# Channel-major delta-rule keys scaled by a broadcast row of reciprocal norms, in place of transposed scaled tokens

## The chip, the cores and the metric

The kernel runs on one core of one Trainium2 chip. The metric is the device time of one execution in microseconds (us); the median of the runs shown is compared. The profile is of one execution of its own, with the span from the first to the last instruction.

## What is computed

One hybrid decoder layer over 512 tokens: a conditioned RMS norm, one wide input projection, a sliding-window attention branch, a gated delta-rule branch, a gated merge and an output projection. The change lies in the delta rule's keys. There are 16 key heads of 128 channels, shared by 32 value heads. Cut to what the keys need, in chunks of 64 tokens:

```python
d_qkv = causal_conv_silu(d_qkv, conv_w)
dq, dk, dv = jnp.split(d_qkv, [DN_KEY, 2 * DN_KEY], axis=-1)
dk = jnp.repeat(l2_norm(dk.reshape(B, T, DN_K_HEADS, DN_HEAD_K)), rep, axis=2)
...
def l2_norm(x):
    xf = x.astype(jnp.float32)
    return xf * lax.rsqrt(jnp.sum(xf * xf, axis=-1, keepdims=True) + EPS)
...
k_beta = k * beta[..., None]
L = jnp.where(strict, jnp.einsum('bhncd,bhnsd->bhncs', k_beta, k) * decay, 0.0)
t_inv = triangular_solve(eye + L, eye)
```

So each token's key is divided by its norm over the 128 channels, and the normed keys are multiplied with each other (K times K transposed), masked by a decay, and enter a triangular inverse.

## The kernel before, in words

Weights are streamed. Each projection tile (128 output channels by 512 tokens) takes 48 matmuls on TensorE: 16 slices of the input, each in three matmuls (L240 to L242) of weights and activations that are split into a high and a low part. A tile's weights come as one load of 1 MB into `raw` (two buffers, L200). ScalarE makes the high half `whi` (L52), VectorE the low half `wlo` (L53), in two halves per tile; three such halves are kept.

All else is written as Python generators that run beside the tiles. After every second slice, that is after six matmuls, `pump` advances the live generators by one count; `yield n` in a generator gives up n counts. This sets the order in which instructions are recorded. A list scheduler then places them on each engine's queue by its own estimate of readiness, so an instruction may stand somewhat earlier or later than recorded. Each engine runs its queue in order. All loads and stores are issued from one queue, SP's; a load or store whose semaphore isn't there yet holds up what stands behind it.

The change lies in `keys` (L651), one generator for each of the 16 key heads, numbered 0 to 15 here. Keys 0 to 3 come from tiles made during the start, 4 to 15 from their own projection tiles, with tiles of the merge gate between them from key 8 on. The steps of one key:

- the convolution with its activation gives `y`, 128 channels by 512 tokens, with channels in the partitions (L576 to L587);
- four transposes on TensorE bring the tokens into the partitions, `ptk` in PSUM (L274);
- ScalarE sums squares per token (L702), VectorE computes the reciprocal root `rky`, 128 tokens by 4 blocks, in ten small steps (L59 to L64);
- two rows `g_rows` are loaded, each broadcast to 128 partitions, as decay masks `E` (L707), which GpSimd completes with a sum and a selection (L714, L715);
- ScalarE scales the tokens to `k` (L668), which is stored to DRAM as `k_d` (L674);
- four more transposes bring `k` back to channels, `ptkT` in PSUM, and ScalarE copies it to `kT` (L676), which is stored as `kT_d` (L682);
- four matmuls of `kT` with itself give `pkk` (L681); VectorE multiplies it with the two masks (L687), and the results are stored as `lt_d` and `lab_d` (L694, L695).

When keys 0 to 7 are stored, their matrices are loaded as `A` and VectorE solves them, a long series of products and sums (L757, L764) that runs beside the later keys. After all keys the loop over heads reads `kT_d` and `k_d` back. In the rows of the profile "pkk x8" are one key's four matmuls, each of which the profile shows as two.

Of the kernel before, what the change touches and what calls it, by code (L numbers as in the profile page):

```python
# [7 lines left out]
F32 = mybir.dt.float32  # L8
# [3 lines left out]
ALU = mybir.AluOpType  # L12
# [4 lines left out]
P = 128  # L17
T = 512
# [4 lines left out]
KH = 16  # L23
# [13 lines left out]
class Layer:  # L37
# [552 lines left out]
    def deltanet(self):  # L590
        tc, nc, a = self.tc, self.nc, self.a
        dram = self.dram
        self.lt_d = dram.tile([2, 2, 16, 4, HD, HD], F32, name="lt_d")
        self.lab_d = dram.tile([VH, HD, 4, HD], F32, name="lab_d")
        self.ta_d = dram.tile([2, 16, 4, HD, HD], F32, name="ta_d")
        self.ts_d = dram.tile([2, 2, 16, 4, HD, HD], F32, name="ts_d")
        self.kT_d = dram.tile([KH, P, T], F32, name="kT_d")
        self.k_d = dram.tile([KH, P, T], F32, name="k_d")
        self.o_d = dram.tile([VH, P, T], F32, name="o_d")
        with ExitStack() as ps:  # L600
            self.pmm = ps.enter_context(tc.tile_pool(name="pmm", bufs=2, space=PSUM, reuse_waits="tile"))
            self.ptp = ps.enter_context(tc.tile_pool(name="ptp", bufs=2, space=PSUM, reuse_waits="tile"))
            self.gwk = ps.enter_context(tc.tile_pool(name="gwk", bufs=1, reuse_waits="tile"))
            sol1 = ps.enter_context(tc.tile_pool(name="sol1", bufs=1, side="right", reuse_waits="tile"))
            with ExitStack() as sa:
                wk = sa.enter_context(tc.tile_pool(name="dnA", bufs=2, reuse_waits="tile"))
                sol0 = sa.enter_context(tc.tile_pool(name="sol0", bufs=1, reuse_waits="tile"))
                gp = sa.enter_context(tc.tile_pool(name="gates", bufs=1, reuse_waits="tile"))
                self.go(self.gates(gp), 1)
                self.keys_done, self.solve_in = [], {}  # L610
                self.keep_order = True
                for g in range(NST):
                    self.go(self.keys(wk, g, self.acc_k[g]), 10 + 8 * g)
                for j in range(NFIRST):
                    self.merge_gate("mb", j, self.mb_d)
                self.go(self.solve_load(sol0, 0), 1)
                self.go(self.solve_load(sol1, 1), 1)
                s0 = self.paced(self.solve(sol0, 0, nc.vector), 0.82)
                s1 = self.paced(self.solve(sol1, 1, nc.vector), 0.0)
                for kind, j in self.mixed():  # L620
                    if kind == "k":
                        self.go(self.keys(wk, j, self.channel_tile(f"k{j}")), 0)
                    else:
                        self.merge_gate("mb", j, self.mb_d)
                        if j == KT - 3:
                            s0[1] = 1.2
                for j in range(3):
                    self.merge_gate("ma", j, self.ma_d)
                    if s0 not in self.slow:
                        s1[1] = 1.1  # L630
                self.drain_live()
                self.drain_slow(s0)
                self.keep_order = False
                s1[1] = 0.6
            with ExitStack() as sb:
                wk = sb.enter_context(tc.tile_pool(name="dnB", bufs=2, reuse_waits="tile"))
                self.tt = []
                for n in range(4):
                    t = wk.tile([P, NTB, P], F32, tag=f"tt{n}", name=f"tt{n}", bufs=1)
                    nc.gpsimd.memset(t[HD:P, :, 0:HD], 0.0)  # L640
                    self.tt.append(t)
                for g in range(KH):
                    if g == 8:
                        self.drain_slow(s1)
                    self.heads(wk, g)
                for j in range(3, 5):
                    self.merge_gate("ma", j, self.ma_d)
                self.drain_live()
        self.dump("o", self.o_d)

    def keys(self, wk, g, ps):  # L651

        nc = self.nc
        y = wk.tile([P, T], F32, tag="y", name="y", bufs=3)
        yield from self.conv(wk, ps, 16 + g, y)
        yield 2
        pt = self.ptp.tile([P, T], F32, tag="tp", name="ptk")
        self.transpose4(pt, lambda c: y[:, c * P : (c + 1) * P])
        ss = self.sumsq(wk, pt)
        yield 3  # L660
        self.hold = 2
        nc.vector.tensor_scalar(out=ss, in0=ss, scalar1=EPS, scalar2=None, op0=ALU.add)
        rk = self.rsqrt(wk, ss, NTB, "rk")
        E = [self.decay_load(wk, 2 * g + e) for e in range(2)]
        yield 2
        k = wk.tile([P, NTB, P], F32, tag="k", name="k")
        for c in range(NTB):
            nc.scalar.activation(k[:, c, :], pt[:, c * P : (c + 1) * P], AF.Copy, scale=rk[:, c : c + 1])  # L668
        for e in range(2):
            self.decay_mask(E[e], 2 * g + e)  # L670
        yield 3
        pt = self.ptp.tile([P, T], F32, tag="tp", name="ptkT")
        self.transpose4(pt, lambda c: k[:, c, :])
        nc.sync.dma_start(out=self.k_d[g], in_=k.rearrange("p c d -> p (c d)"))  # L674
        kT = wk.tile([P, T], F32, tag="kT", name="kT")
        nc.scalar.copy(out=kT, in_=pt)  # L676
        yield 2
        pk = self.ptp.tile([P, NTB, P], F32, tag="tp", name="pkk")
        for c in range(NTB):
            sl = slice(c * P, (c + 1) * P)  # L680
            nc.tensor.matmul(pk[:, c, :], lhsT=kT[:, sl], rhs=kT[:, sl], start=True, stop=True)  # L681
        nc.sync.dma_start(out=self.kT_d[g], in_=kT)  # L682
        for e in range(2):
            nc.scalar.activation(E[e], E[e], AF.Exp)
        yield 1
        for e in range(2):
            nc.vector.tensor_tensor(out=E[e], in0=pk, in1=E[e], op=ALU.mult)  # L687
        yield 2
        for e in range(2):
            h = 2 * g + e  # L690
            b, hl = h // 16, h % 16
            for k2 in range(2):
                s = slice(k2 * HD, (k2 + 1) * HD)
                nc.sync.dma_start(out=self.lt_d[b, k2, hl].rearrange("c j i -> j c i"), in_=E[e][s, :, s])  # L694
            nc.sync.dma_start(out=self.lab_d[h], in_=E[e][0:HD, :, HD:P])  # L695
        self.keys_done.append(g)
# [8 lines left out]
    def decay_load(self, wk, h):  # L705
        E = wk.tile([P, NTB, P], F32, tag="E", name="E", bufs=4)
        self.nc.sync.dma_start(out=E.rearrange("p c i -> p (c i)"), in_=self.g_rows[h].partition_broadcast(P))  # L707
        return E
# [859 lines left out]
```

## Time and profile before

| what | us |
|---|---|
| median of 3 runs | 2932.36 |
| lowest and highest run | 2931.61, 2937.2 |
| span of the profiled execution | 2929.7 |

The profile's page lists the busy time of the engines (PE is TensorE's matmuls, PEld its weight loads, DVE VectorE, ACT ScalarE, POOL GpSimd), then the chain of work that ended last. Rows of the timeline give the start in us, the duration in us, the engine, the line and operation, then output and inputs; brackets at the end give how long the engine had been idle and what released it. Matmuls overlap, so their durations add up to more than the time between their starts. Rows of groups give the busy time, the mean of one in ns, and the idle time before them with its releaser. SPq rows are the issue of a load or store on SP's queue.

The keys stand between about 160 and 500 us of the span.

### The profile page before, as it was taken

Reading aid. Unit: us, or ns where it says so; the run is one execution under the profiler, and the core shown is the slowest. Engines: PE = TensorE matmul, PEld = TensorE weight load, DVE = VectorE, ACT = ScalarE, POOL = GpSimd, SP = SyncE. Lnnn points to the kernel's source line nnn. Section 1 sums busy time; section 2 is a strip of 40 time slices with the busy share of each in tenths; the row PEclk is TensorE's granted clock in tenths of the full one; section 3 lists DMA queues with packets and bytes.
Section 4 is the critical chain, followed back from the end, with each engine's and each line's share of the span. In section 5 each row is a group of like instructions: output and inputs, shape, how many; then the busy total and the mean of one; then the engine's idle time right before and its main releaser. Section 6 shows DMA issues by size and latency. Waiting matters only on the chain.

```text
span 2929.7 us, 38073 instructions
## 1 busy us (share of the span) xinstructions
PE 2870.6 (98%) x14556; PEld 2351.2 (80%) x14556; DVE 1787.2 (61%) x2915; ACT 1085.1 (37%) x2113; POOL 243.0 (8%) x204
## 2 busy tenths in 40 slices
PE   8899999999999999999999999999999999999988
PEld 6677888888888888888888788888787877888867
DVE  6775998777776545544444553434655655553697
ACT  4355333333334333333333322212343443432343
POOL 0022211100000110000000000000100000000022
PEclk9999999999999999999999999999999999999999
DMA  9747555633334533333332675554322223375562
GB/s 387 281 147 219 163 169 159 203 109 111 125 113 134 160 116 124 115 122 109 123 109 100 235 263 182 186 172 141 105 89 94 85 89 103 119 262 172 173 194 97
DMA packets 175046, 451.11 MB, mean 154 GB/s; under 512 B 72433, under 2 KB 74993, under 8 KB 138897
## 3 DMA queue, kind: packets, MB, share of 16 engines
q1 hardware_dynamic: 174866, 448.70, 46.1%
q8 instruction: 114, 1.87, 0.3%
q14 instruction: 66, 0.54, 0.1%
HBM read 386.95 MB, written 59.45 MB: 152 GB/s over the span
## 4 chain that ended last, share of the span: by engine, by line
PE 84%; DVE 3%; DMA 2%; issue 1%; ACT 1%; POOL 1%; SPq 0%; POOLq 0%; DVEq 0%; ACTq 0%
PE mm L240 24%; PE mm L242 24%; PE mm L241 24%; DVE wlo L53 1%; PE S L1208 1%; PE pv L918 1%; PE po L937 1%; PE O L1259 1%; PE pP L274 1%; PE po L936 1%; PE pd L933 1%; PE pp L908 1%; PE m L241 1%; PE m L242 1%; PE m L240 1%
## 5 line engine op out<-in xcount | busy, mean ns | idle before, releaser
L240 PE MATMUL mm<-hh,whi 128*128 128x512 f32 x2784 | 1130.7, 406 | 2.3 <-ACT whi L52 1.6
L242 PE MATMUL mm<-hh,wlo 128*128 128x512 f32 x2784 | 1089.6, 391 | 1.3 <-DVE wlo L53 1.3
L241 PE MATMUL mm<-hl,whi 128*128 128x512 f32 x2784 | 1087.3, 391 | 0.0
L53 DVE TENSOR_TENSOR wlo<-raw,whi 128x1024 fp32r<-128x1024 f32 (+1 forms) x452 | 554.4, 1229 | 491.5 <-ACT whi L52 481.7
L52 ACT CAST whi<-raw 128x1024 fp32r<-128x1024 f32 (+1 forms) x452 | 470.7, 1044 | 972.9 <-PE mm L241 927.3
L242 PEld LDWEIGHTS mm<-hh,wlo 128*128 128x128 f32 x2784 | 522.6, 188 | 115.1 <-DVE wlo L53 2.2
L240 PEld LDWEIGHTS mm<-hh,whi 128*128 128x128 f32 x2784 | 523.7, 188 | 112.3 <-issue 8.4
L241 PEld LDWEIGHTS mm<-hl,whi 128*128 128x128 f32 x2784 | 524.2, 188 | 98.7 <-issue 0.4
L240 PE MATMUL mm<-oh,whi 128*128 128x512 f32 x512 | 200.6, 393 | 2.6 <-ACT oh L52 1.7
L242 PE MATMUL mm<-oh,wlo 128*128 128x512 f32 x512 | 199.4, 390 | 0.5 <-DVE wlo L53 0.5
L241 PE MATMUL mm<-ol,whi 128*128 128x512 f32 x512 | 199.5, 390 | 0.1
L865 POOL TENSOR_TENSOR qe<-qe,yq 128x512 f32<-128x512 f32 x32 | 51.4, 1624 | 902.7 <-DMA qe<-eg_rows 836.9
L714 POOL TENSOR_TENSOR E<-E,neg_g 128x512 f32<-128x512 f32 x64 | 78.4, 1224 | 476.2 <-DMA E<-g_rows 342.8
L240 PEld LDWEIGHTS mm<-oh,whi 128*128 128x128 f32 x512 | 96.0, 188 | 24.8 <-ACT oh L52 3.0
L241 PEld LDWEIGHTS mm<-ol,whi 128*128 128x128 f32 x512 | 96.1, 188 | 22.2 <-DVE ol L53 1.3
L764 DVE TENSOR_TENSOR A<-A,atmp 128x62 f32<-128x62 f32 (+30 forms) x124 | 112.9, 911 | 1.5
L242 PEld LDWEIGHTS mm<-oh,wlo 128*128 128x128 f32 x512 | 96.1, 188 | 20.9 <-DVE wlo L53 1.3
L757 DVE TENSOR_TENSOR atmp<-A 128x62 f32<-128x62 f32 (+30 forms) x124 | 109.3, 882 | 1.5
L911 DVE SCALAR_TENSOR_TENSOR r<-pp,neg_eg,vt 128x128 f32<-128x128 f32 x96 | 29.2, 346 | 78.8 <-PE pp L908 77.6
L1232 ACT ACTIVATE sm<-sm,mx,rs 128x256 f32<-128x256 f32 (+1 forms) x128 | 71.7, 561 | 3.3 <-DVE mx L1227 3.3
L580 DVE SCALAR_TENSOR_TENSOR yv<-mm,convh,yv 128x511 f32<-128x511 f32 (+2 forms) x96 | 71.5, 745 | 1.6
L241 PE MATMUL m<-wlo,hh 128*128 128x512 f32 x128 | 51.8, 404 | 10.1 <-DVE wlo L53 10.1
(331 smaller groups left out, 3145.6 us busy)
## 6 DMA issues: line engine op xcount, KB each, us to landing
raw<-in_w_ch SPq DMA_DIRECT2D x158, 1024.0 KB
wa<-in_w_ada_ss SPq DMA_DIRECT2D x32, 1024.0 KB
raw<-in_w_od SPq DMA_DIRECT2D x32, 1024.0 KB
E<-g_rows SPq DMA_DIRECT2D x64, 256.0 KB
gw<-in_w_ada_gate SPq DMA_DIRECT2D x16, 1024.0 KB
raw<-in_w_os SPq DMA_DIRECT2D x16, 1024.0 KB
qe<-eg_rows SPq DMA_DIRECT2D x32, 256.0 KB
o_d<-zh SPq DMA_DIRECT2D x32, 256.0 KB
```

What stands on the lines that cost most here:

```text
L52: self.nc.scalar.copy(out=hi, in_=src)
L53: self.nc.vector.tensor_tensor(out=lo, in0=src, in1=hi.bitcast(F32), op=ALU.subtract)
L240: nc.tensor.matmul(ps, lhsT=wh, rhs=xh, start=first, stop=False)
L241: nc.tensor.matmul(ps, lhsT=wh, rhs=xl, start=False, stop=False)
L242: self.last_mm = nc.tensor.matmul(ps, lhsT=wl, rhs=xh, start=False, stop=last).ins
L274: self.nc.tensor.transpose(dst[:, c * P : (c + 1) * P], src_cols(c), self.ident)
L580: nc.vector.scalar_tensor_tensor(out=y[:, s:], in0=ps[:, : T - s], scalar=w[:, j : j + 1], in1=y[:, s:], op0=ALU.mult, op1=ALU.add)
L714: nc.gpsimd.tensor_tensor(out=E, in0=E, in1=ng, op=ALU.add)
L757: eng.tensor_tensor(out=t, in0=A[:, m : m + 1, m + 1 :].to_broadcast([P, m, n]), in1=A[:, :m, m : m + 1].to_broadcast([P, m, n]), op=ALU.mult,
L764: eng.tensor_tensor(out=A[:, :m, m + 1 :], in0=A[:, :m, m + 1 :], in1=t, op=ALU.add)
L865: nc.gpsimd.tensor_tensor(out=qf, in0=qf, in1=q, op=ALU.mult)
L1232: nc.scalar.activation(t, t, AF.Exp, scale=r[:, h : h + 1], bias=mx[:, h : h + 1], accum_out=den[:, h : h + 1])
```

## The change

The channel-major key `kT` is no longer made by transposing the scaled tokens. `rk`, the reciprocal norms, is stored to a row of 512 numbers in DRAM, `r_d`, with tokens in order. That store has 512 pieces of one number each. The row is loaded back, broadcast to 128 partitions, into `kT`. GpSimd multiplies it in place with `y`, the unscaled channel-major key. The four transposes `ptkT`, their PSUM tile and ScalarE's copy are gone. The scaled tokens `k` are still made by ScalarE and stored. The store of `k` is recorded two counts after the scaling instead of three; the counts from the reciprocal root to `pkk` are seven, as before. The load of `kT` must wait for the store of `r_d`, which waits for the reciprocal root.

```diff
@@ deltanet
+        self.r_d = dram.tile([KH, T], F32, name="r_d")
@@ keys
         rk = self.rsqrt(wk, ss, NTB, "rk")
+        nc.sync.dma_start(out=self.r_d[g].rearrange("(c p) -> p c", p=P), in_=rk)
         E = [self.decay_load(wk, 2 * g + e) for e in range(2)]
+        kT = wk.tile([P, T], F32, tag="kT", name="kT")
+        nc.sync.dma_start(out=kT, in_=self.r_d[g].partition_broadcast(P))
         yield 2
         k = wk.tile([P, NTB, P], F32, tag="k", name="k")
         for c in range(NTB):
             nc.scalar.activation(k[:, c, :], pt[:, c * P : (c + 1) * P], AF.Copy, scale=rk[:, c : c + 1])
         for e in range(2):
             self.decay_mask(E[e], 2 * g + e)
+        yield 2
+        nc.gpsimd.tensor_tensor(out=kT, in0=kT, in1=y, op=ALU.mult)
+        nc.sync.dma_start(out=self.k_d[g], in_=k.rearrange("p c d -> p (c d)"))
         yield 3
-        pt = self.ptp.tile([P, T], F32, tag="tp", name="ptkT")
-        self.transpose4(pt, lambda c: k[:, c, :])
-        nc.sync.dma_start(out=self.k_d[g], in_=k.rearrange("p c d -> p (c d)"))
-        kT = wk.tile([P, T], F32, tag="kT", name="kT")
-        nc.scalar.copy(out=kT, in_=pt)
-        yield 2
         pk = self.ptp.tile([P, NTB, P], F32, tag="tp", name="pkk")
```

## The prediction

> **What bounds the kernel now.** I read the page first: busy time, then the chain of work that ended last. TensorE fills the span.
>
> ```profile
> span 2929.7 us, 38073 instructions
> PE 2870.6 (98%) x14556; PEld 2351.2 (80%) x14556; DVE 1787.2 (61%) x2915; ACT 1085.1 (37%) x2113; POOL 243.0 (8%) x204
> PE 84%; DVE 3%; DMA 2%; issue 1%; ACT 1%; POOL 1%; SPq 0%; POOLq 0%; DVEq 0%; ACTq 0%
> ```
>
> The reader is to see that work taken off TensorE's queue shortens the kernel one for one, and that any wait put into that queue lengthens it one for one. The edit lies between 160 and 500 us; in the built order of the changed kernel every engine's instructions from the query heads on stand as before. So only this stage counts. Its last stretch, from the table by stage (length in us, then PE, PEld, DVE, ACT and POOL busy):
>
> ```profile
> 450.00:500.00 50.00, 49.14 (x229) 40.37 (x228) 47.79 (x65) 18.86 (x36) 10.74 (x12) 1.00 0.55 165
> ```
>
> PE is nearly full, and so is DVE, which runs the triangular solve there and has 2 us in 50 left.
>
> **What is removed.** Sixteen keys lose four transposes each (ptkT) and a copy on ScalarE. The grouped rows of 160 to 500 us give ptkT's idle time, and POOL's price for the kind of product that is added:
>
> ```profile
> L274 PE MATMUL ptkT<-ident,k 128*128 128x128 f32 x64 | 12.1, 287 | 4.5 <-ACT k L668 4.3
> L714 POOL TENSOR_TENSOR E<-E,neg_g 128x512 f32<-128x512 f32 x32 | 43.7, 1365 | 403.9 <-DMA E<-g_rows 334.9 <-DVE rky L64 54.5 <-DMA k_d<-k 9.4
> ```
>
> Matmuls overlap, so the duration is not the price; the spacing is. Undisturbed matmuls start 0.227 us apart (three steps from 310.90 to 311.58); around four transposes it is 0.91 us from 300.87 to 301.78 for two steps.
>
> ```profile
> 300.87 0.40 PE L242 MATMUL mm<-hh,wlo 128*128 128x512 f32 x1
> 301.11 0.60 PE L274 MATMUL ptkT<-ident,k 128*128 128x128 f32 x4
> 301.46 0.48 PE L240 MATMUL mm<-hh,whi 128*128 128x512 f32 x1
> 301.78 0.40 PE L241 MATMUL mm<-hl,whi 128*128 128x512 f32 x1
> ...
> 310.90 0.39 PE L240 MATMUL mm<-hh,whi 128*128 128x512 f32 x1
> ...
> 311.58 0.39 PE L240 MATMUL mm<-hh,whi 128*128 128x512 f32 x1
> ```
>
> So four transposes cost 0.91 - 0.45 = 0.46 us, and sixteen keys 7.3 us. With them go the 4.5 us that PE stood idle before ptkT, waiting for ScalarE's scaled tokens. Together 11.8 us. The copy of kT on ScalarE (about 0.6 us each) saves nothing by itself: ScalarE is busy 37%. The freed PSUM buffer I count at nothing too, as no row shows a matmul waiting for it.
>
> **What is added, and where it waits.** Before, pkk needed rsqrt, scaling, transposes, copy. Now it needs rsqrt on DVE, a store of the row r_d, a load that waits on SP until the store has landed, and a product on POOL behind the two masks of the same key. PE is in order: if kT is late, pkk and all weight matmuls behind it stand. The prices, from the SP queue's rows, the chain and the timeline:
>
> ```profile
> 314.58 1.25 SPq L694 DMA_DIRECT2D lt_d<-E  x2
> 222.98 2.41 DMA lab_d<-E
> 2918.83 3.39 DMA x<-in_x
> 196.33 0.88 SPq L707 DMA_DIRECT2D E<-g_rows  x2
> 200.27 1.05 POOL L714 TENSOR_TENSOR E<-E,neg_g 128x512 f32<-128x512 f32 x1 [8.68 <-DMA E<-g_rows]
> 410.90 0.90 SPq L707 DMA_DIRECT2D E<-g_rows  x2
> 416.67 1.05 POOL L714 TENSOR_TENSOR E<-E,neg_g 128x512 f32<-128x512 f32 x1 [18.80 <-DMA E<-g_rows]
> ...
> 475.83 2.01 POOL L714 TENSOR_TENSOR E<-E,neg_g 128x512 f32<-128x512 f32 x1
> ```
>
> The store is of 512 single numbers. Two lt_d stores, 256 runs each, take 1.25 us to issue, a run being one contiguous piece; lab_d, 256 runs, lands 2.41 us after its issue began. With another 0.6 us of issue I take 3.05 us; below, 2.41 us; above, 4.2 us, about an E pair's landing. The load is the same shape as one of the E loads: the first of a pair is used 3.94 us after issue (196.33 to 200.27), 5.77 us when a weight load is ahead of it (410.90 to 416.67), and a plain load of that size took 3.39 us. I take 3.94, the same kind without company. The product: 1.37 us mean, 1.05 to 2.01 at the ends. With 0.15 us for the hand-overs, rsqrt's end to pkk needs 8.5 us; bounds 6.9 and 12.
>
> What is there for it? One undisturbed late key, with the last rsqrt step and pkk:
>
> ```profile
> 349.56 0.60 PE L274 MATMUL ptk<-ident,y 128*128 128x128 f32 x4
> 356.82 0.16 DVE L64 SCALAR_TENSOR_TENSOR rky<-rkt,rky 128x4 f32<-128x4 f32 x1
> 364.12 1.05 PE L681 MATMUL pkk<-kT 128*128 128x128 f32 x8
> ```
>
> 7.1 us, less 0.46 for the transposes that are gone: 6.7. Here the built order keeps pkk behind the same weight matmul as before. For others it moves pkk: counted in weight matmuls of 0.227 us, by +9, +8, -6, +6, +2, +8 for keys 0 to 5, by 39 to 52 for keys 6 to 8 and 36 for key 9, and by 0, 0, +7, 0, 0, +17 for keys 10 to 15. The rows of keys 0, 1, 2, 5, 14 and 15:
>
> ```profile
> 178.99 0.16 DVE L64 SCALAR_TENSOR_TENSOR rky<-rkt,rky 128x4 f32<-128x4 f32 x1
> 179.61 1.10 PE L274 MATMUL ptkT<-ident,k 128*128 128x128 f32 x4 [1.00 <-ACT k L668]
> 183.74 1.05 PE L681 MATMUL pkk<-kT 128*128 128x128 f32 x8
> 193.13 0.16 DVE L64 SCALAR_TENSOR_TENSOR rky<-rkt,rky 128x4 f32<-128x4 f32 x1
> 193.75 0.33 PE L274 MATMUL ptkT<-ident,k 128*128 128x128 f32 x1 [0.77 <-ACT k L668]
> 197.54 1.05 PE L681 MATMUL pkk<-kT 128*128 128x128 f32 x8
> 206.83 0.16 DVE L64 SCALAR_TENSOR_TENSOR rky<-rkt,rky 128x4 f32<-128x4 f32 x1
> 216.31 1.05 PE L681 MATMUL pkk<-kT 128*128 128x128 f32 x8
> 235.97 0.16 DVE L64 SCALAR_TENSOR_TENSOR rky<-rkt,rky 128x4 f32<-128x4 f32 x1
> 236.58 0.59 PE L274 MATMUL ptkT<-ident,k 128*128 128x128 f32 x2 [1.68 <-ACT k L668]
> 240.03 1.05 PE L681 MATMUL pkk<-kT 128*128 128x128 f32 x8
> 450.37 0.16 DVE L64 SCALAR_TENSOR_TENSOR rky<-rkt,rky 128x4 f32<-128x4 f32 x1
> 456.84 1.05 PE L681 MATMUL pkk<-kT 128*128 128x128 f32 x8
> 476.86 1.00 DVE L64 SCALAR_TENSOR_TENSOR rky<-rkt,rky 128x4 f32<-128x4 f32 x1
> 478.32 1.10 PE L274 MATMUL ptkT<-ident,k 128*128 128x128 f32 x4 [0.86 <-ACT k L668]
> 482.03 1.05 PE L681 MATMUL pkk<-kT 128*128 128x128 f32 x8
> ```
>
> Room is the gap from rsqrt's end to pkk, plus the move, less 0.46, less the idle in brackets (it goes, so PE is there sooner). Key 0: 4.59 + 2.04 - 0.46 - 1.00 = 5.2, so 3.3 us are missing. Key 1: 4.25 + 1.82 - 0.46 - 0.77 = 4.8; 3.7 missing. Key 2: 9.32 - 1.36 - 0.46 = 7.5; 1.0. Key 5: 3.90 + 1.82 - 0.46 - 1.68 = 3.6; 4.9. Key 14: 6.31 - 0.46 = 5.85; 2.65. Key 15: 4.17 + 3.86 - 0.46 - 0.86 = 6.7; 1.8. Keys 10 and 13 have key 11's distance and aren't moved: 1.8 each with it. For key 12 the move leaves 0.3, but its mask loads now stand behind the waiting store, and I take 1.5. Keys 3, 4 and 6 to 9 I put at nothing: 3 and 4 have key 2's distance and a move to the good, the others the longer one. Sum 12.9 for keys 0 to 5 and 11.4 for 10 to 15: 24 us of new standing on PE.
>
> The store waits on SP for rsqrt, the load for the store. Behind them stand kT_d, k_d, the next key's mask loads and weight loads. In the late part the weight loads wait anyway, for DVE to free a raw buffer:
>
> ```profile
> SPq L200 <- DVE wlo L53: 95.9, 15, 12.9
> ```
>
> (15 times between 150 and 540 us, up to 12.9 us). So I count nothing for SP; without that cover a weight load 3 to 4 us later per key would cost up to that. POOL's product may also hold DVE up: the last rsqrt step of key 15 took 1.00 us beside POOL work, 0.16 elsewhere, at most 16 x 0.85 = 13.6 us. PE's new waits give DVE that time back, so nothing.
>
> **The sum.** -11.8 + 24 = +12 us on the profiled 2929.7: a span of 2942. The median of the runs lies 2.7 us above that span, so about 2944 us. With the round trip at 6.9 us, each tight key stands 1.6 us less: about 9 us in all, net -3. At 12 us keys 2 to 4 join, about 60 us, net +48.
>
> **Rivals.**
> *The round trip hides* (faster). The order was built with a readiness for kT that put most pkk where they were; if that is right, nothing new stands, and -11.8 gives 2920.5 us. For it: keys 6 to 9 were moved far, so lateness was reckoned with. Against: keys 0, 1 and 5 have under 5.3 us, and the fastest two transfers seen already take 5.8 without the product.
> The Trainium skill ("DMA: Bandwidth & Descriptors", Anatomy of one DMA) gives a transfer about 2.0 us fixed plus its bytes at 436 GB/s; my estimate from it is 2.0 + 2.6 + 1.37 = 6.0 us, which leaves some 4 us of standing and about 2925 us. The same page (Specifications) says that pieces under 512 B cost a read-modify-write, which speaks for a slower store; no row here has a piece of 4 B.
>
> *SP becomes the bound in the middle* (slower). Keys 3 to 8 follow each other closely, and in the built order of that part the weight load stands right behind kT_d, which waits for POOL's product, and the mask loads that POOL needs first stand behind r_d, which waits for rsqrt. Decides if kT of keys 5 to 8 is more than about 5 us later than the order assumes; each weight tile late by 5 to 6 us, four tiles, adds 20 to 24 us: 2966 us. Against: the longer distance of pkk there moves with it.
>
> *Even* (no change that can be told). Store and load at their fast ends: -3, 2929 us.
>
> **How the numbers follow.** Forecast 0.55, hidden 0.13, SP 0.20, even 0.12. A change under about 0.2%, 6 us, can't be told from none. Faster: 0.14 (hidden, and a little of even). Same: 0.17 (the rest of even, the low edge of the forecast). Slower: 0.69. Predicted 2944. The range reaches down into even, 2925, and above over the SP case, 2970; the forecast's own is 2930 to 2962.
>
> **What would show it.** Right: PE's ptkT rows gone; idle before pkk, released by POOL's kT product, 15 to 30 us in about ten keys, largest at keys 0, 1, 5 and 14; r_d landing about 3 us after issue, the load about 4. Wrong in size: pkk idle under 8 us (hidden), or the store landing after 5 us or more. Wrong in kind: PE idle at the weight matmuls released by ScalarE's or DVE's split, which wait for raw loads (SP).

## The result and the profile after

| | kernel before | changed kernel |
|---|---|---|
| median of the runs, us | 2931.99 (4 runs, 2929.86 to 2937.2) | 3088.01 (4 runs, 3086.12 to 3090.3) |
| span of the profiled execution, us | 2929.7 | 3085.6 |

The changed kernel is slower: 1.0536 times the time of before, 95% interval 1.0521 to 1.0551. That is 156 us, where 12 were forecast.

The page of the changed kernel, first the busy time, then the granted clock in 40 slices (each digit is tenths of full speed), then the chain of work that ended last, by engine:

```profile
PE 2898.9 (94%) x14492; PEld 2373.6 (77%) x14492; DVE 1788.8 (58%) x2915; ACT 1078.3 (35%) x2097; POOL 247.7 (8%) x220
PEclk9988888899999999999999999999999999999999
PE 78%; DMA 9%; DVE 7%; ACT 2%; POOL 2%; issue 1%; SPq 0%; POOLq 0%; DVEq 0%; ACTq 0%
```

The reader is to see two things that the page of before did not have: the chain, which was TensorE nearly throughout, now runs through transfers for 9% of the span, and the clock stands below 0.9 for six slices of 77 us, from about 154 us on.

Where does the extra time stop growing? The last key's pkk answers that:

```profile
637.53 2.08 PE L682 MATMUL pkk<-kT 128*128 128x128 f32 x8 [12.56 <-POOL kT L676]
```

Before, that row stood at 482.03 us. The shift is 155.5 us; the rest of the kernel takes 2448.1 us against 2447.7. So all of it lies in the stage of the keys. The table by stage splits it (length, then PE, PEld, DVE, ACT and POOL busy, the clock, the share of the DMA engines, GB/s); the stretch ends 2.5 us behind the last pkk in both. First the changed kernel:

```profile
160.00:640.00 480.00, 345.86 (x1453) 282.34 (x1452) 265.36 (x432) 137.08 (x322) 88.27 (x84) 0.85 0.50 128
```

The kernel before:

```profile
160.00:484.50 324.50, 316.52 (x1503) 259.62 (x1502) 259.61 (x427) 142.94 (x337) 73.61 (x68) 1.00 0.57 176
```

PE stands for 480.0 - 345.9 = 134.1 us, against 8.0 before: 126.2 us more. It is also busy 29.3 us longer, although transposes worth 7.3 us are gone. So the matmuls that are left take 36.6 us longer: 126.2 + 36.6 - 7.3 = 155.5. Not all of the 36.6 us is slowness: the stretch holds 12 more weight matmuls (1255 against 1243), because the last pkk stands later in the order; at 0.227 us each that is 2.7 us, and about 34 us are left. The groups of that stretch say which (busy time, mean of one in ns, idle before it and its releaser), in the changed kernel:

```profile
L240 PE MATMUL mm<-hh,whi 128*128 128x512 f32 x419 | 173.9, 415 | 1.6 <-ACT whi L52 1.6
L242 PE MATMUL mm<-hh,wlo 128*128 128x512 f32 x418 | 171.8, 411 | 1.3 <-DVE wlo L53 1.3
...
L682 PE MATMUL pkk<-kT 128*128 128x128 f32 x128 | 31.4, 423 | 127.6 <-POOL kT L676 127.6
```

and before:

```profile
L240 PE MATMUL mm<-hh,whi 128*128 128x512 f32 x415 | 165.8, 399 | 1.6 <-ACT whi L52 1.6
L242 PE MATMUL mm<-hh,wlo 128*128 128x512 f32 x414 | 162.2, 392 | 1.3 <-DVE wlo L53 1.3
...
L681 PE MATMUL pkk<-kT 128*128 128x128 f32 x128 | 16.9, 275 | 0.0
```

The standing is all in one row: 127.6 us before pkk, released by GpSimd's product. The weight matmuls wait for the weight splits no longer than before (1.6 and 1.3 us). pkk itself is busy nearly twice as long.

One key, followed along the chain, from the last step of the reciprocal root to pkk (start, duration, what):

```profile
409.78 1.00 DVE rky L64
...
410.80 8.95 DMA r_d<-rky
...
419.82 5.62 DMA kT<-r_d
...
425.66 1.27 POOL kT L676
...
426.98 2.07 PE pkk L682 x8
429.05 0.43 PE mm L240
...
432.47 0.43 PE mm L242
432.89 0.28 PE mm L240
433.17 0.23 PE mm L241
```

From the root's end (410.78) to pkk it is 16.2 us: 9.0 for the store, 5.8 from the load's issue to the product, 1.3 for the product. The prediction had 3.05, 3.94 and 1.37. Behind the stop nine weight matmuls start 0.43 us apart, and only then they are back at 0.23.

SP's queue waits for the store 16 times before it issues the load (total, times, longest):

```profile
SPq L668 <- DMA r_d<-rky: 142.4, 16, 11.9
```

From the store's issue to the load's issue the 16 keys take 8.8 to 13.9 us, 10.85 in the median. The issue of the store itself takes 0.38 us on SP in most keys, no longer than one of the lt_d stores of 256 pieces (1.25 us for two).

### The profile page after: what moved, and what is told of

It is laid out like the page before. It is cut to its first block, busy times and chain, and to the rows that moved or that the text cites. A ratio compares the mean times of both kernels' runs of the same rounds, so it can differ in the third digit from the quotient of the medians.

```text
span 3085.6 us, 38030 instructions
## 1 busy us (share of the span) xinstructions
PE 2898.9 (94%) x14492; PEld 2373.6 (77%) x14492; DVE 1788.8 (58%) x2915; ACT 1078.3 (35%) x2097; POOL 247.7 (8%) x220
## 4 chain that ended last, share of the span: by engine, by line
PE 78%; DMA 9%; DVE 7%; ACT 2%; POOL 2%; issue 1%; SPq 0%; POOLq 0%; DVEq 0%; ACTq 0%
PE mm L240 22%; PE mm L242 22%; PE mm L241 22%; DMA r_d<-rky 4%; DVE wlo L53 2%; DMA kT<-r_d 1%; DVE wa L414 1%; PE S L1209 1%; PE pv L919 1%; PE po L938 1%; PE O L1260 1%; PE pP L274 1%; PE pkk L682 1%; ACT whi L52 1%; PE po L937 1%
## 5 line engine op out<-in xcount | busy, mean ns | idle before, releaser
L240 PEld LDWEIGHTS mm<-hh,whi 128*128 128x128 f32 x2784 | 530.3, 190 | 114.5 <-issue 8.4
L241 PEld LDWEIGHTS mm<-hl,whi 128*128 128x128 f32 x2784 | 530.4, 191 | 101.0 <-issue 0.4
L682 PE MATMUL pkk<-kT 128*128 128x128 f32 x128 | 31.4, 423 | 127.6 <-POOL kT L676 127.6
L682 PEld LDWEIGHTS pkk<-kT 128*128 128x128 f32 x128 | 26.8, 310 | 134.2 <-POOL kT L676 134.2
L688 DVE TENSOR_TENSOR E<-pkk,E 128x512 f32<-128x512 f32 x32 | 20.9, 686 | 113.0 <-PE pkk L682 49.5
```

The source lines that it names most:

```text
L240: nc.tensor.matmul(ps, lhsT=wh, rhs=xh, start=first, stop=False)
L241: nc.tensor.matmul(ps, lhsT=wh, rhs=xl, start=False, stop=False)
```

## The experiments

Each time stands beside that of the kernel before on the same chip. A time with an interval is the median of several runs; a time without one is a single run. The experiments ran on three chips, so small differences between single runs say little.

### Is it the store, or load and product?

Change: the load reads a row that was stored long before. The store stays, and nobody waits for it.

```diff
-        nc.sync.dma_start(out=kT, in_=self.r_d[g].partition_broadcast(P))
+        nc.sync.dma_start(out=kT, in_=self.eg_rows[g].partition_broadcast(P))
```

> The changed kernel, but the load of kT reads a row of eg_rows that has lain in DRAM since the gates, and so does not wait for the r_d store; the store is still issued. The keys are scaled by that other row. Theory (the store of 512 single numbers is what is late, 9 to 12 us, and the load and the product are not): from the end of rsqrt to pkk 6 to 7.5 us, PE's idle time before pkk, 127.6 us in the changed kernel, under 30 us, time between 2920 and 2960 us. Rival (load and product on GpSimd are as much to blame): idle time over 60 us, time above 2990 us.

Measured: 3010.25 us, before 2929.39. The rival's two numbers came: 78 us are gone, but 81 remain, and PE still stands 65.3 us before pkk. Its reason, a load and a product that are late by themselves, is not what the chain of that run shows (SPq L665 is the issue of the r_d store):

```profile
450.92 0.38 SPq L665
451.35 14.48 DMA E<-g_rows
...
465.97 1.04 POOL E L715
...
469.45 1.25 POOL kT L676
470.74 2.07 PE pkk L682 x8
```

The mask load E, issued right behind the store, lands after 14.5 us. In the prediction's rows such a load was in use 3.9 to 5.8 us after its issue. The product waits on GpSimd behind the masks, and pkk behind it. By 453.3 us SP had issued both mask loads, the load of kT and one more store behind the r_d store, and the issue of the next, of `k_d`, then held SP for 9.71 us. Meanwhile the DMA engines moved next to nothing (columns as in the table by stage; the last two are the share of the DMA engines and GB/s):

```profile
452.20:462.00 9.80, 8.12 (x36) 6.38 (x34) 5.83 (x5) 2.11 (x2) 0.00 (x0) 1.00 0.12 6
```

That gave a new theory: the store delays whatever is behind it on the queue. A run in which the store's pieces lie 64 B apart in DRAM (rs_d, 16 numbers for each token) tests that:

```diff
-        nc.sync.dma_start(out=self.r_d[g].rearrange("(c p) -> p c", p=P), in_=rk)
+        nc.sync.dma_start(out=self.rs_d[g, :, 0].rearrange("(c p) -> p c", p=P), in_=rk)
```

> The run with the other row (kT's load reads eg_rows and waits for no store; 3010 us, 65 us of standing before pkk), but with the r_d store spread to 64 B between its pieces (rs_d). The keys are again scaled by that other row. Theory (the standing in that run came from transfers behind the packed store on the queue): idle before pkk under 15 us, time 2925 to 2945 us. Rival (load and product come too late for pkk even without any store in front): idle over 30 us, time above 2960 us.

Measured: 2946.11 us, before 2933.49; a microsecond above the expected range, and 64 us faster than with the packed store. On every engine the instructions of the stage stand in the same order as in the run before, so the distance of the pieces is what differs. The mask load of the same key, the DMA engines behind the store, and the row of pkk:

```profile
398.56 5.00 DMA E<-g_rows
...
399.40:404.40 5.00, 5.00 (x23) 4.13 (x22) 3.57 (x4) 1.86 (x2) 0.71 (x1) 1.00 0.86 159
...
L682 PE MATMUL pkk<-kT 128*128 128x128 f32 x128 | 19.4, 299 | 8.7 <-POOL kT L676 8.7
```

The mask load lands after 5.0 us instead of 14.5, with the DMA engines 0.86 busy instead of 0.12, and 8.7 us of standing are left. Load and product are hardly late when the store ahead of them is spread out.

### The store alone, in the kernel before

Change: one line in the kernel before; nothing reads r_d.

```diff
         rk = self.rsqrt(wk, ss, NTB, "rk")
+        nc.sync.dma_start(out=self.r_d[g].rearrange("(c p) -> p c", p=P), in_=rk)
```

> The kernel before, with the r_d store added behind rsqrt on SP and nothing that reads it. Theory (the store costs only him who waits for it): the time of the kernel before within 6 us. Rival (the store, waiting for rsqrt on SP, holds up the mask and weight loads behind it, or its small pieces hold up other transfers): 10 to 40 us slower without any wait for r_d.

Measured: 2970.45 us, before 2929.39. The rival was right in time within a microsecond, 41 us. It had named two reasons, SP's wait for the reciprocal root and small pieces that hold up other transfers, and these had to be parted. The chain of this run:

```profile
193.37 0.55 SPq L665
193.97 12.31 DMA lab_d<-E
...
419.43 0.38 SPq L665
419.86 13.97 DMA E<-g_rows
```

The store of lab_d, issued 0.6 us behind r_d, lands after 12.31 us; before, the prediction's row had 2.41. The same store with 64 B between its pieces, in the same built order:

```diff
+        nc.sync.dma_start(out=self.rs_d[g, :, 0].rearrange("(c p) -> p c", p=P), in_=rk)
```

> The kernel before with an added store behind rsqrt that nothing reads, as in the run with the store alone (2970 us against 2929), in the same built order, but its 512 pieces of 4 B lie 64 B apart (rs_d), the form that landed in about 1.9 us in the run with four forms. Theory (the 41 us come from the ten microseconds for which the tightly packed store holds up the transfers behind it): 2929 to 2942 us. Rival (they come from SP, which waits for rsqrt with the mask and weight loads behind it): 2962 to 2975 us, as with the packed store.

Measured: 2940.47 us, before 2932.13, ratio 1.0029 (1.0019 to 1.0038), in the theory's range. Its chain:

```profile
219.25 3.68 DMA lab_d<-E
223.02 3.83 DMA E<-g_rows
```

So of the 41 us, a single run, some 33 come from the close packing of the pieces, and 8 from the store as such, most likely from its issue and SP's wait for the root.

### What makes the store slow

Change: four forms of the store, by key; each load waits for its own.

```diff
+        if g % 4 == 0:
+            nc.sync.dma_start(out=row.rearrange("(c p) -> p c", p=P), in_=rk)
+        elif g % 4 == 1:
+            nc.sync.dma_start(out=row.rearrange("(p c) -> p c", p=P), in_=rk)
+        elif g % 4 == 2:
+            nc.sync.dma_start(out=self.rs_d[g, :, 0].rearrange("(c p) -> p c", p=P), in_=rk)
+        else:
+            nc.vector.tensor_copy(out=self.rw[:, 0:4], in_=rk)
+            nc.vector.transpose(out=rt, in_=self.rw)
+            for b in range(4):
+                nc.sync.dma_start(out=self.rl_d[g, :, b, :], in_=rt[32 * b : 32 * b + 4])
```

> The changed kernel with four forms of the store, key by key: keys 0, 4, 8, 12 as it is, 512 pieces of 4 B (r_d); keys 1, 5, 9, 13 128 pieces of 16 B (rp_d); keys 2, 6, 10, 14 512 pieces of 4 B, each 64 B from the next (rs_d); keys 3, 7, 11, 15 after a transpose of 32x32 blocks on VectorE four stores of four pieces of 128 B (rl_d). Each load waits for its own store; keys of the second form get their norms in another order, keys of the third a row that is mostly other data. Theory (the number of tiny pieces makes the store late): from the store's issue to the load's issue 9 to 11 us for r_d, the same for rs_d if the count alone matters and under 7 us if neighbours in DRAM are what costs, 3 to 5 us for rp_d, 2 to 3 us for rl_d; time 3000 to 3040 us. Rival (any write to DRAM that is then read takes that long, or the store waits behind other traffic): 8 to 11 us for all four, time about 3088 us.

Measured: 2987.64 us, before 2929.39, which is below the range that was expected. SP's queue for the last key of each form; the load is issued when its store has landed:

```profile
424.00 0.38 SPq L674 DMA_DIRECT2D r_d<-rky  x1
...
433.86 0.32 SPq L690 DMA_DIRECT2D kT<-r_d  x1
...
461.92 0.32 SPq L677 DMA_DIRECT2D rp_d<-rky  x1
463.36 0.32 SPq L690 DMA_DIRECT2D kT<-rp_d  x1
...
499.83 0.37 SPq L680 DMA_DIRECT2D rs_d<-rky  x1
501.75 0.32 SPq L690 DMA_DIRECT2D kT<-rs_d  x1
...
530.48 1.27 SPq L687 DMA_DIRECT2D rl_d<-rt  x4
...
532.89 0.32 SPq L690 DMA_DIRECT2D kT<-rl_d  x1
```

Packed numbers 9.86 us (all four keys 8.5 to 11.8), 128 pieces of 16 B 1.44 us, 512 numbers 64 B apart 1.92 us, four stores of 128-byte pieces 2.41 us. The theory's count of pieces fell here: the third form has the same 512 pieces of 4 B as the first. What differs is how near they lie. The keys in the middle take longer in the other forms (rs_d 8.08 us for key 6, rp_d 6.07 for key 5), with a weight load of 1 MB issued 0.5 and 3.2 us ahead.

Next the distance was varied; s is the number of places from piece to piece, and for s = 1 only one number of each partition is stored:

```diff
+            s = (2, 4, 8, 1)[g % 4]
+            nc.sync.dma_start(out=d[:, 0].rearrange("(c p) -> p c", p=P), in_=rk)
...
+            nc.sync.dma_start(out=d[0:P], in_=rk[:, 0:1])
```

> The changed kernel with the distance of the 4-byte pieces in DRAM changed key by key: keys 0, 4, 8, 12 512 pieces 8 B apart (r8_d), keys 1, 5, 9, 13 16 B apart (r16_d), keys 2, 6, 10, 14 32 B apart (r32_d), keys 3, 7, 11, 15 only 128 pieces, side by side (r1_d). The loads read a row of that tensor that is mostly other data. Theory (pieces that lie close together wait for each other): from the store's issue to the load's issue, where no weight load is ahead, 6 to 9 us at 8 B, 3 to 6 us at 16 B, 2 to 3 us at 32 B, and 2 to 4 us for the 128 pieces side by side. Rival (the closeness plays no part, traffic made the difference): no order among the distances.

Measured: 2993.86 us, before 2932.13. SP's queue for keys 12, 13 and 14:

```profile
433.93 0.38 SPq L671 DMA_DIRECT2D r_d<-rky  x1
...
438.85 0.32 SPq L676 DMA_DIRECT2D kT<-r_d  x1
...
465.68 0.37 SPq L671 DMA_DIRECT2D r_d<-rky  x1
...
468.38 0.32 SPq L676 DMA_DIRECT2D kT<-r_d  x1
...
502.78 0.37 SPq L671 DMA_DIRECT2D r_d<-rky  x1
504.82 0.32 SPq L676 DMA_DIRECT2D kT<-r_d  x1
```

| distance of the 4-byte pieces | pieces in 64 B | store's issue to load's issue, us |
|---|---|---|
| 4 B | 16 | 9.86 |
| 8 B | 8 | 4.92 (key 0: 4.47) |
| 16 B | 4 | 2.70 (key 1: 2.70) |
| 32 B | 2 | 2.04 (key 2: 2.22) |
| 64 B | 1 | 1.92 |

The first and the last row are from the run with four forms. The order of the distances came out as expected; at 8 B and 16 B the times are below the expected ones. The time follows the closeness: on average 0.5 us for each further piece in 64 B, (9.86 - 1.92) / 15, little for the second (2.04 - 1.92) and 0.6 for each of the last eight. The 64 B are the measure of the table; how long the stretch is in which pieces delay each other isn't shown. The keys left out of the table had more transfers just ahead. The 128 pieces side by side took 8.8 us in key 11, which had nothing closer ahead of it than keys 13 and 14 of the table, and 11.1 to 12.7 in the other three; 2 to 4 were expected. So a quarter of the pieces, as close together, is nearly as late as all 512, and it is the closeness that counts and not the number. Which part of the memory path makes the pieces wait isn't shown.

### The change with a better store

Change: the row is stored in 16-byte pieces (a partition's four norms side by side), and the product reads it in that order, in place in y. The built order is that of the changed kernel within a few matmuls.

```diff
-        nc.sync.dma_start(out=self.r_d[g].rearrange("(c p) -> p c", p=P), in_=rk)
+        nc.sync.dma_start(out=self.r_d[g].rearrange("(p c) -> p c", p=P), in_=rk)
...
-        nc.gpsimd.tensor_tensor(out=kT, in0=kT, in1=y, op=ALU.mult)
+        ch = y.rearrange("d (c p) -> d c p", c=NTB)
+        nc.gpsimd.tensor_tensor(out=ch, in0=kT.rearrange("d (p c) -> d c p", c=NTB), in1=ch, op=ALU.mult)
+        kT = y
```

> The changed kernel with the row stored as 128 pieces of 16 B (four norms of a partition side by side) and GpSimd's product reading it in that order, in place in y. The built order is that of the changed kernel within a few matmuls. Theory (with a store that lands in 1.5 to 2.5 us the round trip is the 8.5 us of the prediction, and nothing is held up behind it): idle time before pkk 15 to 45 us instead of 127.6, time 2932 to 2958 us. Rival (most of the loss lies in the round trip as such, in SP or in GpSimd): above 2980 us.

Measured: 2972.64 us, before 2932.13, ratio 1.0137 (1.0122 to 1.0152). The standing before pkk came as expected; the time lies between the theory's range and the rival's:

```profile
L684 PE MATMUL pkk<-y 128*128 128x128 f32 x128 | 23.3, 339 | 26.7 <-POOL y L677 26.2 <-ACT k L672 0.5
```

The last pkk stands at 527.6 us, 45.6 later than before; the profiled execution is the slowest of the four runs. From 160 us to 2.5 us behind it PE is busy 330.5 of 370.1 us: it stands 39.6 - 8.0 = 31.6 us longer, 26.7 of it before pkk, and its remaining matmuls take 330.5 - 316.5 + 7.3 = 21.3 us longer. 31.6 + 21.3 - 7.3 = 45.6. Of the 21.3 us, 4.1 are 18 more weight matmuls in the stretch, so some 17 go to slower ones. From the store's issue to the load's it is 1.6 to 2.4 us in seven keys, but 3.4 to 9.6 in nine, most of them in the middle, with other transfers just ahead. The product takes 1.5 to 2.5 us in its new order of reading. With such a round trip the standing before pkk is 26.7 us.

The variant with rows in token order, copied and transposed in blocks of 32x32 on VectorE and stored as 16 pieces of 128 B in four transfers:

```diff
+        nc.vector.tensor_copy(out=self.rw[:, 0:NTB], in_=rk)
+        nc.vector.transpose(out=rt, in_=self.rw)
+        rows = self.r_d[g].rearrange("(c b i) -> c b i", c=NTB, b=4)
+        for b in range(4):
+            nc.sync.dma_start(out=rows[:, b, :], in_=rt[32 * b : 32 * b + NTB])
```

> The changed kernel with the row brought into order on VectorE (a copy and a transpose of 32x32 blocks) and stored as 16 pieces of 128 B in four transfers. Theory: as with 16-byte pieces, later by the two operations and the four issues, about 1.5 us a key: 2945 to 2975 us. Rival: above 2985 us.

Measured: 2959.88 us, before 2932.13, with 20.1 us of standing before pkk. This is within the range. The order isn't the same, though: in 14 of the 16 keys pkk stands 6 to 15 weight matmuls later than in the changed kernel, which gives each round trip 1.4 to 3.4 us more room.

### The clock

The granted clock can be read around the stop of the key that was followed above: in the changed kernel pkk starts at 426.98 us, after 11.13 us of standing (columns as in the table by stage, the clock being the third number from the end):

```profile
427.00:432.80 5.80, 5.80 (x18) 4.93 (x19) 3.65 (x6) 0.00 (x0) 0.00 (x0) 0.50 0.36 128
432.90:440.00 7.10, 7.10 (x34) 5.86 (x34) 5.76 (x7) 1.97 (x5) 0.00 (x0) 1.00 0.11 28
```

Half the clock is granted for 5.9 us of work, until the very matmul from which the spacing is 0.23 us again. In the run with 16-byte pieces the stops of three keys and what pkk takes behind them (the bracket is the stop):

```profile
359.16 1.76 PE L684 MATMUL pkk<-y 128*128 128x128 f32 x8 [2.19 <-POOL y L677]
...
388.70 2.08 PE L684 MATMUL pkk<-y 128*128 128x128 f32 x8 [4.50 <-POOL y L677]
...
495.52 1.16 PE L684 MATMUL pkk<-y 128*128 128x128 f32 x8 [1.65 <-POOL y L677]
```

In the profiles of all these runs, pkk takes 1.13 to 1.16 us behind a stop of 0.4 to 1.96 us, and 1.6 to 2.1 us behind one of 3.4 us or more, with one exception (1.17 us behind 4.03); between 1.99 and 3.4 us both occur. Two runs fill the stops with work that is thrown away. First in the changed kernel, 880 transposes:

```diff
         pk = self.ptp.tile([P, NTB, P], F32, tag="tp", name="pkk")
+        for n in range((80, 65, 71, 15, 41, 22, 15, 20, 40, 35, 77, 89, 77, 71, 75, 87)[g]):
+            nc.tensor.transpose(pk[:, n % 4, :], self.ident, self.ident)
```

> The changed kernel with 15 to 89 transposes of the identity into pkk's PSUM tile ahead of pkk's own matmuls, for each key about 0.8 of the time for which PE stood there (840 transposes, some 97 us in all); their results are overwritten. Theory (37 of the 155 us come from the granted clock, which falls when PE stands for long): pkk's eight matmuls take about 1.1 us instead of 2.0, the clock of the stage rises from 0.85 to above 0.95, and although PE is given more work the time falls to 3050 to 3068 us. Rival (the slower matmuls come from something else, or the clock falls with the late store however PE is kept): 3080 us or more.

Measured: 3095.1 us, before 2929.39. The theory missed, and the rival's number came: no time was won.

```profile
L681 PE MATMUL pkk<-ident 128*128 128x128 f32 x880 | 101.0, 276 | 4.8 <-ACT k L672 4.8
L684 PE MATMUL pkk<-kT 128*128 128x128 f32 x128 | 25.0, 357 | 50.0 <-POOL kT L676 50.0
```

The filling took 101 us and left 50 us of stops, most of them above 3.5 us: the built order moved pkk, and for keys 6 to 9 the transposes stand well ahead of it. But the clock of the stage rose from 0.85 to 0.94, and the rest of PE's work took 422.6 - 101.0 = 321.6 us instead of 345.9. Of these 24.3 us, 4.8 are 21 weight matmuls that the stretch no longer holds; some 19.5 of the 34 us were bought back, and paid for with filling that took 25 us more than the standing it replaced (58.3 us of standing are left of 134.1). Second, the same with 140 transposes in six stops of the kernel with 16-byte pieces:

```diff
+        for n in range({0: 18, 10: 12, 11: 30, 12: 30, 13: 18, 15: 32}.get(g, 0)):
+            nc.tensor.transpose(pk[:, n % 4, :], self.ident, self.ident)
```

> The kernel with the 16-byte pieces (2973 us, six stops of over 2 us before pkk), with 12 to 32 transposes of the identity ahead of pkk's matmuls for keys 0, 10, 11, 12, 13 and 15, 140 in all (some 16 us), sized to leave under 2 us of each stop; their results are overwritten. Theory (behind a stop of over 3 us the matmuls take up to twice as long for 5 us, some 2.9 us a stop): pkk takes 1.05 to 1.2 us for these keys, and the time falls by 8 to 17 us, to 2956 to 2965 us, though PE has more to do. Rival (the clock's part is small): 2970 us or more.

Measured: 2981.59 us, before 2933.49, ratio 1.0169 (1.0152 to 1.0186): a miss again, in the rival's range and no faster than without filling. In the stage, PE's other work fell from 330.5 to 333.7 - 16.3 = 317.4 us, 13.1 less, of which 6.4 are 28 weight matmuls that the stretch no longer holds; but 16.3 us of filling were added, and 22.8 us of standing before pkk stayed, as the built order put pkk earlier, by 9 weight matmuls for key 0 and 16 for key 15. Both runs show a part of the clock's price in PE's busy time; neither shows it as time won.

### Hiding what is left

pkk can be put later. In the changed kernel, with eight more steps between product and pkk:

```diff
-        yield 3
+        yield 11
         pk = self.ptp.tile([P, NTB, P], F32, tag="tp", name="pkk")
```

> The changed kernel as it is, store of 512 single numbers included, with eight more steps of waiting between the product and pkk; pkk stands 27 to 61 weight matmuls (6 to 14 us) later for most keys. Theory (the packed store also holds up what stands behind it, so hiding the round trip wins back the standing before pkk but not that): idle before pkk 10 to 50 us, time 2965 to 3015 us. Rival (only the wait before pkk costs): below 2950 us.

Measured: 3035.74 us, before 2931.61. Standing before pkk fell from 127.6 to 40.1 us as expected, but 33.2 us appeared before the transposes ptk, and the time stayed above the theory's range: a packed store costs more than the wait for it, and more than the theory allowed. The better stores with three more steps, `yield 6`, first with the 16-byte pieces:

> The kernel with the 16-byte pieces (2973 us) with three more steps of waiting between the product and pkk; in the built order pkk stands 9 to 18 weight matmuls (2 to 4 us) later for keys 0, 1, 3, 5 and 9 to 14, but only 1 for key 15. Theory (what is left of the loss there is 26 us of PE standing before pkk and the low clock behind each stop of over 3 us): the idle time before pkk falls to 6 to 12 us, the pkk groups take 1.1 us, time 2940 to 2955 us. Rival (the rest of the loss stands elsewhere, at the weight splits and SP): above 2960 us.

Measured: 2960.82 us, before 2931.61, ratio 1.0103 (1.0088 to 1.0118). The standing before pkk fell to 10.2 us as expected; the time fell by 12 us only, in the rival's range, as the standing before the weight matmuls grew from 7.0 to 14.7 us, released by VectorE's convolution and by the weight splits. Then with the store issued by ScalarE's queue instead of SP's:

```diff
-        nc.sync.dma_start(out=self.r_d[g].rearrange("(p c) -> p c", p=P), in_=rk)
+        nc.scalar.dma_start(out=self.r_d[g].rearrange("(p c) -> p c", p=P), in_=rk)
```

> As the run before, with the r_d store issued on ScalarE's queue instead of SP's, so that SP no longer waits for rsqrt. Theory (SP's wait costs the 8 us by which the spaced store alone was slower than the kernel before): 5 to 10 us less than the run before, 2932 to 2948 us. Rival (ScalarE stands for rsqrt and splits weights later instead): no less than the run before, or more.

Measured: 2946.28 us, before 2931.61, ratio 1.0054 (1.0035 to 1.0073), 14.5 less than the run before, where 5 to 10 were expected. SP's wait for the root, 49.6 us in the run before, is gone, but its wait for the store grew from 18.9 to 54.3 us; so that a shorter wait on SP is the reason is likely, and not shown. And the 128-byte pieces with `yield 6`:

> The kernel with 16 pieces of 128 B (2960 us) with three more steps of waiting before pkk, which stands 2 to 4 us later for most keys, 0.2 us earlier for key 15. Theory: its 19 us of idle time before pkk fall to under 8 us, time 2937 to 2950 us. Rival: above 2955 us.

Measured: 2945.79 us, before 2931.61, ratio 1.0049 (1.0034 to 1.0064). The time is in the range; the standing before pkk, under 8 us by the theory, is not:

```profile
L689 PE MATMUL pkk<-kT 128*128 128x128 f32 x128 | 19.0, 294 | 14.2 <-POOL kT L683 12.3 <-ACT k L679 1.7
```

No version beat the kernel before; the two best are 14 us slower than it, with 14.2 us of standing left before pkk here.

## Why the prediction was right in sign and wrong in size

**What is removed** held: the ptkT rows are gone, and with them their 4.5 us of idle time, though PE now stands 3.6 us before the transposes ptk instead of 0.6. The 7.3 us for the transposes themselves is taken over from the prediction in the sums here; no run measured it apart.

**The price of the store** is the step that failed first. The prediction wrote: "With another 0.6 us of issue I take 3.05 us; below, 2.41 us; above, 4.2 us". It was 8.8 to 13.9 us. The estimate came from rows of stores with contiguous runs of 256 B, as the nearest there were, and so treated the store as so many pieces; it took the long issue (1.25 us for two such stores) for the sign of their cost. The issue was 0.38 us, and the lateness came behind it. Not the number of pieces made it late, nor their size (512 pieces of 4 B landed in 1.92 us when 64 B apart), but how close they lie, 16 of them in 64 B. The Trainium skill's sentence that was weighed there ("DMA: Bandwidth & Descriptors", Specifications: transfers under 512 B cost a read-modify-write) pointed to a slower store; by itself it does not part the two forms, which are both of 4 B. The fixed 2.0 us of the Trainium skill ("DMA: Bandwidth & Descriptors", Anatomy of one DMA), given there for transfers that GpSimd issues, are near the 1.92 us of the spread store, issued by SP, and far from the packed one.

**The load**, from its issue to the product, took 3.5 to 8.3 us over the 16 keys, 5.15 in the median, above the 3.94 taken, and near the 5.77 that the prediction had from a load with company; **the product**, 1.27 us in 15 keys, was right. The upper bound of 12 us for the round trip was too low: 16.2 us for the key followed, and 14.6 to 20.3 from the store's issue to the product's end over all keys.

**The room for each key** came out near in sum, and that was luck. With the row in 16-byte pieces PE stood 26.7 us before pkk; the prediction had 24 us. But keys 0 to 5 stood 5.9 us where 12.9 were forecast, and keys 10 to 15 20.8 where 11.4 were: for key 5 4.9 us were forecast and none was measured, for key 11 1.8, and 4.5 were measured. Nor was the round trip the 8.5 us of the prediction: from the store's issue to the product's end it took 8.3 to 15.1 us there.

**"So I count nothing for SP"** failed, in a way that none of the rivals had. The prediction thought of what stands behind the waiting store on SP. That costs little: 8 us for a spread store in the kernel before. What it did not think of is what stands behind the store on the DMA engines once it is issued: masks and results landing after 12 to 14 us, which cost some 33 us in the kernel before with no one reading the row. The Trainium skill ("DMA: Bandwidth & Descriptors", Queues, rings and completion order) says that each DMA engine takes the descriptors of one queue in ring order, though a later one may finish its write before an earlier one. The late lab_d and E agree with the order: behind the packed store the engines moved 6 GB/s with loads already issued. How they would treat a transfer of another queue, no run here shows. The rival that put the loss at late weight tiles falls: PE waits 2.9 us for weight splits, as before.

**The clock** was not in the sum at all. The prediction's "any wait put into that queue lengthens it one for one" failed: a microsecond of standing cost more than a microsecond. In the changed kernel 126 us of added standing brought about 34 us of slower matmuls, in the kernel with 16-byte pieces 31.6 brought some 17. For the one key of the chain above, pkk took 2.07 us and nine weight matmuls 0.43 instead of 0.23 us. The Trainium skill ("TensorE: Matmul & The Clock Gate", Part 1) has this: after an idle window of about 3.4 us the array runs at half its clock, until it has been busy about as long. The halving agrees: the granted clock was 0.50, and 0.43 is about twice 0.227. The times agree less well: stops of 2.0 to 3.4 us were followed by slow matmuls in some keys too, and it took 5.9 us of work until the clock was back in the key followed.

**The sum.** Of the 156 us, 115 go with the packing of the store (3088.0 to 2972.6 us in nearly the same built order), with its own lateness, the transfers held up behind it and the clock that follows. The other 40.5 (45.6 by the profiled execution, the slowest of its four) are 26.7 us of standing before pkk, 4.9 us of other standing and 21.3 us by which the remaining matmuls of the stretch took longer, some 17 of it by the clock, less the 7.3 us of transposes. So about a quarter of the loss remains with a good store, and the sign of the prediction does not hang on the packing alone. The rivals *hides* and *even* fall with the store. Among the signs that the prediction named for a wrong size, "the store landing after 5 us or more" is what the trace showed.

What stays open: why close pieces wait for each other, and what the last 14 us of the two best versions are made of beyond the standing that their rows name.

## What to carry to other kernels

A store that scatters single numbers next to each other is priced by how many fall into the same short stretch of memory, and it delays the loads and stores issued right behind it on the same queue, also when no one reads it. Spread the pieces, or put a partition's numbers side by side, before judging a round trip through DRAM. And when TensorE sets the time, price a stop of over 3 us at its length plus some 3 us of slow matmuls behind it (pkk 1.0 us longer and nine weight matmuls 0.2 us each, in the key followed); a stop of up to 1.96 us cost pkk nothing here.

## What the runs showed of the hardware that was not expected

- A store of 512 pieces of 4 B from 128 partitions: 9.9 us when adjoining, 4.9 at 8 B, 2.7 at 16 B, 2.0 at 32 B, 1.9 at 64 B; 128 pieces of 16 B, adjoining, 1.4 us; 128 pieces of 4 B, adjoining, 8.8 us (each in a key with nothing just ahead).
- Transfers issued just behind the adjoining form land after 12.3 to 14.5 us, where 2.4 to 5.8 us were seen without it. The DMA engines show no work that would tell of it: behind one such store they were 0.12 busy for 9.8 us, against 0.86 for 5 us behind the spread form in the same order.
- Issuing the 512 pieces took SP 0.38 us.
- A stop of 4.5 us was followed by pkk at 2.08 us, one of 1.65 us by pkk at 1.16 us. Behind a stop of 11.13 us the granted clock was 0.50 for 5.9 us of work.
